# The modulation of a hybrid layer: weight pieces first, all of them split, rows turned by transposition, context and latent tokens loaded behind

## The chip, the cores and the metric

The kernel runs on one core of one Trainium2 chip. The metric is the device time of one execution in microseconds (us), as the median of several runs. Five engines matter here, each with an instruction queue that it works off in order: PE (matmul, with its weight loads shown as PEld), DVE, ACT, POOL and SP. SP issues DMAs; ACT can issue them too, on a queue of its own.

## The reference, cut to what matters

One layer over 2048 latent tokens (`x`) and 256 context tokens (`ctx`), 1024 channels. Everything behind these lines (a gated delta rule in chunks, windowed attention, the merge) is the same before and after.

```python
shift, scale, gate = split(silu(c) @ w_mod + b_mod, 3)        # w_mod 1024 x 3072, float32
shift_c, scale_c, _ = split(silu(c_ctx) @ w_mod + b_mod, 3)
h  = rmsnorm(x, norm_w) * (1 + scale) + shift                 # latent tokens
hc = rmsnorm(ctx, norm_w) * (1 + scale_c) + shift_c           # context tokens
p_c = hc @ w_in[:, :N_STATE]                                  # the state columns of both
p   = h  @ w_in[:, :N_STATE]
```

## The kernel before, in words

**Precision by splitting.** A float32 matrix `w` is cut in two fp32r parts, `hi` (a cast, on ACT or POOL) and `lo = w - hi` (a subtraction on DVE), and the products of the parts are summed in PSUM. A product in plain float32 needs no split, but PE takes two passes for it.

**Start (L60 to L63, L254 to L278).** SP loads the identity (`ident`), then the rows of c, c_ctx, norm_w and b_mod into one 40 x 128 tile (L260). PE turns that tile (L262), DVE copies it to `craw` (L264), ACT takes the tanh (L268) and DVE makes silu of both conditions: `sil4` (hi and lo of the two, four columns) and `silz` (float32).

**Modulation (L303 to L334).** For j = 0 (shift) and j = 1 (scale) come eight pieces `wm` of w_mod, 128 x 1024 float32 (512 KB) each, nine buffers. Six of eight are split: ACT casts `wmh` (L314), DVE subtracts `wml` (L315), PE multiplies `sil4` by both parts (L318, four matmuls of 512 columns). Pieces 3 and 7 (`WHOLE`) go to PE as they are (L310). The products lie in PSUM as four rows (the two conditions by hi, and by lo). ACT and DVE copy them to `mrow` (L325), eight small float32 matmuls against `sel` add the hi and lo rows and turn them to columns (L328), and DVE adds the bias (L330) and makes `modB` (j = 0, L332) and `modA` = (1 + scale) * norm_w (j = 1, L334).

**Context in between.** Behind pieces 4 and 6 of j = 0 the two context tiles are loaded (`load_x`, L283) and normalised (`norm_x`: half the squares on ACT L292, half on DVE L295, a small L296, the power of -0.5 on POOL L72, and the scaling of the tile on DVE L298).

**h (make_h, L336 to L347).** For every two of eight k: PE transposes the normalised tiles (L343), ACT applies modA and modB (L344, `h32`, two buffers), POOL makes the hi part (L346), DVE the lo part (L347).

**State products.** `tm_weights` loads the 272 state columns of w_in in eight pieces (`wr`, 136 KB, three buffers, L364), ACT casts (L365), DVE subtracts (L366). `tm_dense` is 24 matmuls for 128 tokens (L373 to L375) into one of three PSUM buffers. `state_pair` (L428 to L474) takes two such results, normalises and rotates the keys (DVE L433, L437, L438, L442, L457, L461, L464, L465; POOL L72, L451, L460; PE L471) and spills.

**Order of the stage.** First the context: make_h, state_pair. Then eight groups of 256 latent tokens (L490): load two x tiles (four `xt` buffers with the context), norm_x, make_h, tm_dense, state_pair. Then the qkv products begin (L542), and PE is busy until the end. A planner orders each engine's queue when the kernel is built, in program order but with instructions pulled ahead where it expects the earlier ones to wait; `tc.issue_after(r)` keeps the instructions of its block behind `r` in that order. Before, the state weights and the x tiles stand behind the last w_mod piece in this way, and the norms of group 0 behind `rows_out`, the copies of L325.

Of the kernel before, what the change touches and what calls it, by code (L numbers as in the profile page):

```python
# [7 lines left out]
F32 = mybir.dt.float32  # L8
# [9 lines left out]
KT = D // 128  # L18
# [10 lines left out]
def f32(ap):  # L29
    return ap.bitcast(F32)  # L30
# [10 lines left out]
def _hybrid(ctx, tc, nc, V, S, G, T, ins, out, dbg, upto):  # L41
# [19 lines left out]
    dma(ident, ins["k_mats"][0])  # L61
    identr = cst.tile([128, 128], F32R, name="identr")
    V.tensor_copy(identr, ident)  # L63
# [188 lines left out]
    if True:  # L252
# [5 lines left out]
        for r, n, src in ((0, 8, ins["c"]), (8, 8, ins["c_ctx"].rearrange("(o n) -> o n", o=1)),  # L258
                          (16, 8, ins["norm_w"]), (24, 16, ins["b_mod"][:, 0:2 * D])):
            dma(rows[r:r + n], src.rearrange("o (k p) -> (o k) p", p=128))  # L260
# [3 lines left out]
        V.tensor_copy(craw, cols)  # L264
        cc_ = craw[:, 0:16].rearrange("p (c k) -> p k c", c=2)
# [11 lines left out]
        sel = pm.tile([4, 2], F32, name="sel")  # L277
        V.tensor_tensor(sel, ident[0:4, 0:2], ident[0:4, 2:4], op=ALU.add)  # L278

        def load_x(c):  # L280
            xt = px.tile([128, D], F32, name="xt")
            src = ins["ctx"][0, c * 128:(c + 1) * 128] if c < NCB else ins["x"][0, (c - NCB) * 128:(c - NCB + 1) * 128]
            dma(xt, src)  # L283
            return xt
# [15 lines left out]
        pre = []  # L300
        WHOLE = (3, 7)
        modT = pm.tile([128, 16, 2], F32, name="modT")
        for j in range(2):  # L303
            mps = [psum("acc" if n == 0 else "hps", [4, 512], name=f"mps{n}") for n in range(2)]
            for k in range(KT):
                wm = pm.tile([128, D], F32, name="wm", bufs=9)
                wm_dma = dma(wm, ins["w_mod"][0, k * 128:(k + 1) * 128, j * D:j * D + D])
                if k in WHOLE:
                    for n in range(2):
                        T.matmul(mps[n], lhsT=silz[:, k], rhs=wm[:, n * 512:(n + 1) * 512], start=False, stop=k == KT - 1)  # L310
                    continue
                wmh = pm.tile([128, D], F32R, name="wmh", bufs=3)
                wml = pm.tile([128, D], F32R, name="wml", bufs=3)
                S.copy(wmh, wm)  # L314
                V.tensor_tensor(wml, wm, f32(wmh), op=ALU.subtract)  # L315
                for w in (wmh, wml):
                    for n in range(2):
                        T.matmul(mps[n], lhsT=sil4[:, k], rhs=w[:, n * 512:(n + 1) * 512],  # L318
                                 start=k == 0 and w is wmh, stop=False)
                if j == 0 and k in (4, 6):  # L320
                    c = k // 2 - 2
                    pre.append(load_x(c))
                    norm_x(c, pre[c])
            mrow = pm.tile([4, D], F32, name="mrow", tag="wm", bufs=9)
            rows_out = [(V.tensor_copy if n % 2 else S.copy)(mrow[:, n * 512:n * 512 + 512], mps[n]) for n in range(2)]  # L325
            mtp = psum("kt", [128, 8, 2], name="mtp")
            for i in range(8):
                T.matmul(mtp[:, i], lhsT=mrow[:, i * 128:i * 128 + 128], rhs=sel, start=True, stop=True)  # L328
            mt = modT[:, j * 8:j * 8 + 8]
            V.tensor_tensor(mt, mtp, bm[:, j * 8:j * 8 + 8].unsqueeze(2).to_broadcast([128, 8, 2]), op=ALU.add)  # L330
            if j == 0:
                V.tensor_copy(modB, mt)  # L332
            else:
                V.scalar_tensor_tensor(modA, mt, 1.0, nw.unsqueeze(2).to_broadcast([128, KT, 2]), op0=ALU.add, op1=ALU.mult)  # L334

        def make_h(xts, hi, lo, cc):  # L336
            n = len(xts) * 128
            for k in range(0, KT, 2):
                h32 = px.tile([128, 2, 256], F32, name="h32", bufs=2)
                for i in range(2):  # L340
# [3 lines left out]
                    S.activation(h32[:, i, :n], ps[:, :n], AF.Identity, scale=modA[:, k + i, cc:cc + 1],  # L344
# [1274 lines left out]
```

## Time and profile before

| | us |
|---|---|
| median of 3 runs | 1978.22 (1977.2 to 1982.95) |
| the profiled execution's own time | 1983.69 |
| its span (first to last instruction) | 1982.0 |
| granted TensorE clock, mean | 0.993 |
| modA written | 37.50 |
| first state product (tmps) | 39.74 |
| first qkv product (lps) | 133.68 |

How to read it: in the timeline a row has the start, the time from the first start to the last end of the merged instructions, engine, line, operation, output <- inputs, count, and in brackets how long the engine was idle before and what ended that. In the table by stretches each engine has its busy time and the count, then the granted clock of PE, the busy share of the DMA engines and the GB/s.

### The profile page before, as it was taken

To read this page: it belongs to the slowest core of one execution; us is meant where nothing else is said; L and a number is where in the kernel's file an instruction comes from. 1 tells how busy PE (TensorE), PEld (TensorE's weight loads), DVE (VectorE), ACT (ScalarE), POOL (GpSimd) and SP (SyncE) were. 2 spreads that over 40 slices of the span, in tenths; PEclk is the share of its full clock that TensorE was granted. 3 is DMA by queue.
4 is the path that set the end of the run, shared out by engine and by line. 5 is a ranking of instruction groups with operands and counts; after the bars stand their busy time and mean duration, and the time that the engine had idled before them with its cause. 6 is when DMAs were issued, how large, how long until landed. Compare 5 with 4: busy or idle time off the path is not lost. (4 is left out here: it accounts for less than half of the span.)

```text
span 1982.0 us, 32091 instructions
## 1 busy us (share of the span) xinstructions
PE 1911.1 (96%) x10947; PEld 1601.1 (81%) x10947; DVE 1505.9 (76%) x2869; ACT 803.8 (41%) x1994; POOL 706.7 (36%) x768
## 2 busy tenths in 40 slices
PE   7899999999999999999999999999999999999898
PEld 3788888788998787887888888788878888877686
DVE  6979766777776899999778776545786878757888
ACT  5745545554444322211122233324775656532321
POOL 2642111234543201104222333323555343422675
PEclk9999999999999999999999999999999999999999
DMA  7552326765546633537887777755555555455453
GB/s 264 174 139 85 98 88 158 181 169 159 162 145 164 188 111 113 149 97 214 224 244 229 226 222 218 200 162 186 156 181 173 184 164 159 122 174 195 145 168 134
DMA packets 387703, 333.12 MB, mean 168 GB/s; under 512 B 83992, under 2 KB 307536, under 8 KB 386900
## 3 DMA queue, kind: packets, MB, share of 16 engines
q1 hardware_dynamic: 352244, 288.60, 50.0%
q10 hardware_dynamic: 35296, 42.48, 6.2%
q8 instruction: 87, 1.43, 0.3%
q14 instruction: 76, 0.62, 0.1%
HBM read 220.28 MB, written 109.13 MB: 166 GB/s over the span
## 5 line engine op out<-in xcount | busy, mean ns | idle before, releaser
L542 PE MATMUL rps<-hh,wh 128*128 128x512 f32 x768 | 308.9, 402 | 5.4 <-DVE rt L836 4.2
L544 PE MATMUL rps<-hh,wl 128*128 128x512 f32 x768 | 306.8, 400 | 0.0
L543 PE MATMUL rps<-hl,wh 128*128 128x512 f32 x768 | 306.7, 399 | 0.0
L581 DVE SCALAR_TENSOR_TENSOR cacc<-y,cw,cacc 128x512 f32<-128x512 f32 (+1 forms) x224 | 162.7, 747 | 21.6 <-ACT cacc L579 17.8
L542 PEld LDWEIGHTS rps<-hh,wh 128*128 128x128 f32 x768 | 144.9, 189 | 41.1 <-DVE rt L836 5.3
L542 PE MATMUL lps<-hh,wh 128*128 128x512 f32 (+1 forms) x448 | 171.9, 384 | 0.3 <-ACT y L652 0.3
L543 PE MATMUL lps<-hl,wh 128*128 128x512 f32 (+1 forms) x448 | 171.6, 383 | 0.0
L544 PEld LDWEIGHTS rps<-hh,wl 128*128 128x128 f32 x768 | 144.8, 188 | 32.8
L544 PE MATMUL lps<-hh,wl 128*128 128x512 f32 (+1 forms) x448 | 170.9, 382 | 0.0
L543 PEld LDWEIGHTS rps<-hl,wh 128*128 128x128 f32 x768 | 144.8, 189 | 31.6
L962 DVE TENSOR_TENSOR pl<-pt,ph 128x512 fp32r<-128x512 f32 x156 | 105.6, 686 | 45.0 <-ACT ph L960 43.9
L960 ACT CAST ph<-pt 128x512 fp32r<-128x512 f32 x156 | 90.6, 585 | 109.2 <-PE pt L958 71.7
L834 ACT ACTIVATE rt<-rps 128x512 f32<-128x512 f32 x96 | 57.3, 597 | 181.8 <-PE rps L544 158.2
L934 DVE CUSTOM_DVE_ANT_0 pr<-sc,band,sk 128x640 f32<-128x640 f32 (+1 forms) x128 | 106.7, 862 | 19.4 <-PE sc L930 12.1
L944 POOL TENSOR_SCALAR pr<-pr,sm 128x640 f32<-128x640 f32 (+1 forms) x128 | 101.4, 811 | 56.0 <-DVE sm L942 39.2
L765 DVE TENSOR_TENSOR btmp<-N 128x62 f32<-128x62 f32 (+30 forms) x124 | 116.2, 937 | 3.1
L767 DVE TENSOR_TENSOR N<-N,btmp 128x62 f32<-128x62 f32 (+30 forms) x124 | 116.1, 936 | 3.0
L246 DVE TENSOR_TENSOR wl<-wr,wh 128x512 fp32r<-128x512 f32 x120 | 95.2, 806 | 25.6 <-POOL wh L245 24.1
L936 ACT ACTIVATE pr<-pr,sm 128x640 f32<-128x640 f32 (+1 forms) x128 | 104.1, 815 | 23.3 <-DVE sm L934 23.3
L245 POOL TENSOR_SCALAR wh<-wr 128x512 fp32r<-128x512 f32 x72 | 48.6, 689 | 167.4 <-PE lps L543 97.1
L1249 PE MATMUL pps<-yh,wph 128*128 128x512 f32 x256 | 105.4, 414 | 2.3 <-DVE tb L1260 1.7
L1251 PE MATMUL pps<-yh,wpl 128*128 128x512 f32 x256 | 101.4, 397 | 1.6 <-POOL wpl L1211 1.6
(379 smaller groups left out, 5035.4 us busy)
## 6 DMA issues: line engine op xcount, KB each, us to landing
wr<-in_w_in_dram SPq DMA_DIRECT2D x120, 256.0 KB
kw<-Ksp SPq DMA_DIRECT2D x28, 384.0 KB
x<-vsp SPq DMA_DIRECT2D x36, 256.0 KB
k<-ksp SPq DMA_DIRECT2D x34, 256.0 KB
kT<-kTsp SPq DMA_DIRECT2D x34, 256.0 KB
wm<-in_w_mod_dram SPq DMA_DIRECT2D x16, 512.0 KB
xt<-in_x_dram SPq DMA_DIRECT2D x16, 512.0 KB
dtl<-Dsp SPq DMA_DIRECT2D x32, 256.0 KB
```

Source lines behind the costliest of these rows:

```text
L542: T.matmul(ps, lhsT=wh[:, k], rhs=xh[:, k], start=k == 0, stop=False)
L543: T.matmul(ps, lhsT=wh[:, k], rhs=xl[:, k], start=False, stop=False)
L544: T.matmul(ps, lhsT=wl[:, k], rhs=xh[:, k], start=False, stop=k == kt - 1)
L581: V.scalar_tensor_tensor(a, y[:, t:t + n], cw[:, m, t:t + 1], a, op0=ALU.mult, op1=ALU.add)
L765: V.tensor_tensor(tv, A[:, m + 1:, m].unsqueeze(2).to_broadcast([h1 + n, r, m]), A[:, m, 0:m].unsqueeze(1).to_broadcast([h1 + n, r, m]), o ...
L767: V.tensor_tensor(A[:, m + 1:, 0:m], A[:, m + 1:, 0:m], tv, op=ALU.add)
L934: V.tensor_tensor_reduce(s_, ps[:, o:768], band[:, b0:b0 + W + 256], -0.125, sk[:, 1, hd:hd + 1], ALU.add, ALU.min, sm[:, h, 1:2])
L936: S.activation(s_, s_, AF.Exp, scale=-1.0, bias=sm[:, h, 1:2], accum_out=sm[:, h, 2:3])
L944: G.tensor_scalar(p[:, h, :W + 256], p[:, h, :W + 256], sm[:, h, 3:4], 1.0, op0=ALU.mult, op1=ALU.mult)
L962: V.tensor_tensor(pl, pt, f32(ph), op=ALU.subtract)
L1249: T.matmul(ps, lhsT=wh[:, k, ms], rhs=hs[k], start=k == 0, stop=False)
L1251: T.matmul(ps, lhsT=wl[:, k, ms], rhs=hs[k], start=False, stop=k == 3)
```

## The change

- **First issues.** The first w_mod piece is SP's first DMA. The rows of c, c_ctx and norm_w go on ACT's queue; b_mod and the identity follow on SP's, behind the first piece.
- **All pieces split**, but the first half of the very last (float32 product). PE multiplies a piece's hi part at once and its lo part one piece later; `sel` goes.
- **Rows to columns** by eight transpositions against the identity, and DVE adds the hi and lo columns. The 1 of (1 + scale) is added to the bias at the start. The rows of j = 0 are copied out behind the first piece of j = 1, their columns made behind its third.
- **Order of loads.** Context tiles behind the last w_mod piece, the state weights behind the context, x behind the state weights; five `wr` buffers for three.
- **Order of work.** Context norms stand behind the columns of j = 1. The norms of groups 0 and 1 stand behind the second pair of the make_h before (ACT and DVE part), and POOL's turning of the k norm weights behind the last hi part of the context.

The diff, cut (the moved lines of the start are left out):

```diff
+        def load_w(j, k):
+            wm = pm.tile([128, D], F32, name="wm", bufs=9)
+            return wm, dma(wm, ins["w_mod"][0, k * 128:(k + 1) * 128, j * D:j * D + D])
+
+        wm0 = load_w(0, 0)
+        for q, r, n, src in ((adma, 0, 8, ins["c"]), (adma, 8, 8, ins["c_ctx"].rearrange("(o n) -> o n", o=1)),
+                             (adma, 16, 8, ins["norm_w"]), (dma, 24, 16, ins["b_mod"][:, 0:2 * D])):
+            q(rows[r:r + n], src.rearrange("o (k p) -> (o k) p", p=128))
+        dma(ident, ins["k_mats"][0])
...
+        V.tensor_scalar(craw[:, 32:40], craw[:, 32:40], 1.0, None, op0=ALU.add)
...
+        def mod_product(j, k, w, ns=(0, 1), stop=()):
+            for n in ns:
+                T.matmul(mps[j][n], lhsT=(silz if w.dtype == F32 else sil4)[:, k], rhs=w[:, n * 512:(n + 1) * 512],
+                         start=k == 0 and w.name.startswith("wmh"), stop=n in stop)
+        def mod_rows(j):
+            mrow = pm.tile([4, D], F32, name="mrow", tag="wm", bufs=9)
+            for n, copy in enumerate((S.copy, V.tensor_copy)):
+                copy(mrow[:, n * 512:n * 512 + 512], mps[j][n])
+            return mrow
+        def mod_columns(j, mrow):
+            mtp = psum("kt", [128, 8, 4], name="mtp")
+            for i in range(8):
+                T.transpose(mtp[:, i], mrow[:, i * 128:i * 128 + 128], ident[0:4, 0:4])
+            mt = modT[:, j * 8:j * 8 + 8]
+            V.tensor_tensor(mt, mtp[:, :, 0:2], bm[...], op=ALU.add)
+            V.tensor_tensor(modB if j == 0 else mt, mt, mtp[:, :, 2:4], op=ALU.add)
+            if j == 1:
+                V.tensor_tensor(modA, mt, nw[...], op=ALU.mult)
...
             for k in range(KT):
-                if k in WHOLE:
-                    for n in range(2):
-                        T.matmul(mps[n], lhsT=silz[:, k], rhs=wm[:, n * 512:(n + 1) * 512], start=False, stop=k == KT - 1)
-                    continue
...
+                last = j == 1 and k == KT - 1
+                r = slice(512 if last else 0, D)
+                S.copy(wmh[:, r], wm[:, r])
+                V.tensor_tensor(wml[:, r], wm[:, r], f32(wmh[:, r]), op=ALU.subtract)
+                if last:
+                    mod_product(j, k, wm, (0,))
+                    mod_product(*low, stop=(0,))
+                    mod_product(j, k, wmh, (1,))
+                    mod_product(j, k, wml, (1,), (1,))
+                else:
+                    mod_product(j, k, wmh)
+                    if low:
+                        mod_product(*low, stop=(0, 1) if k == 0 else ())
+                    low = j, k, wml
+                if j == 1 and k == 0:
+                    mrow = mod_rows(0)
+                elif j == 1 and k == 2:
+                    mod_columns(0, mrow)
-                if j == 0 and k in (4, 6):
-                    c = k // 2 - 2
-                    pre.append(load_x(c))
-                    norm_x(c, pre[c])
+        mrow = mod_rows(1)
+        mod_columns(1, mrow)
+        for c in range(NCB):
+            with tc.issue_after(wm_dma.ins):
+                pre.append(load_x(c))
+        ctx_dma = x_dma[0]
+        for c in range(NCB):
+            norm_x(c, pre[c])
...
-                wr = pw.tile([128, NST], F32, name="wr", tag="wr", bufs=3)
+                wr = pw.tile([128, NST], F32, name="wr", tag="wr", bufs=5)
...
-        with tc.issue_after(wm_dma.ins):
+        with tc.issue_after(ctx_dma.ins):
             wh, wl = tm_weights(C_ST, NST)
...
-                with tc.issue_after(wm_dma.ins):
+                with tc.issue_after(wr_dma[0].ins):
                     xts.append(load_x(c))
                 with ExitStack() as behind:
-                    if gi == 0:
-                        for r in rows_out:
-                            behind.enter_context(tc.issue_after(r.ins))
+                    if gi < 2:
+                        for h in made[:2]:
+                            behind.enter_context(tc.issue_after(h.ins))
                     norm_x(c, xts[j])
```

More of the change, by code (lines that the diff above doesn't have):

```diff
@@ L276, in _hybrid @@
         V.tensor_copy(silz[:, :, 0:2], silc)
-        sel = pm.tile([4, 2], F32, name="sel")
-        V.tensor_tensor(sel, ident[0:4, 0:2], ident[0:4, 2:4], op=ALU.add)
+        x_dma = [None]
         def load_x(c):
@@ L298, in norm_x @@
             V.tensor_scalar(xt, xt, rstd[:, c:c + 1], None, op0=ALU.mult)
-        pre = []
-        WHOLE = (3, 7)
         modT = pm.tile([128, 16, 2], F32, name="modT")
+        mps = [[psum("acc" if n == 0 else "hps", [4, 512], name=f"mps{n}") for n in range(2)] for j in range(2)]
+        def mod_product(j, k, w, ns=(0, 1), stop=()):
+            for n in ns:
+                T.matmul(mps[j][n], lhsT=(silz if w.dtype == F32 else sil4)[:, k], rhs=w[:, n * 512:(n + 1) * 512],
+                         start=k == 0 and w.name.startswith("wmh"), stop=n in stop)
@@ L303, in _hybrid @@
+        low = None
         for j in range(2):
-            mps = [psum("acc" if n == 0 else "hps", [4, 512], name=f"mps{n}") for n in range(2)]
             for k in range(KT):
-                wm = pm.tile([128, D], F32, name="wm", bufs=9)
-                wm_dma = dma(wm, ins["w_mod"][0, k * 128:(k + 1) * 128, j * D:j * D + D])
-                if k in WHOLE:
-                    for n in range(2):
-                        T.matmul(mps[n], lhsT=silz[:, k], rhs=wm[:, n * 512:(n + 1) * 512], start=False, stop=k == KT - 1)
-                    continue
+                wm, wm_dma = load_w(j, k) if j + k else wm0
+                last = j == 1 and k == KT - 1
+                r = slice(512 if last else 0, D)
@@ L312, in _hybrid @@
                 wmh = pm.tile([128, D], F32R, name="wmh", bufs=3)
                 wml = pm.tile([128, D], F32R, name="wml", bufs=3)
[L314 to L319, printed above, removed]
-                if j == 0 and k in (4, 6):
-                    c = k // 2 - 2
-                    pre.append(load_x(c))
-                    norm_x(c, pre[c])
@@ L324, in _hybrid @@
[L324 to L334, printed above, removed]
+                S.copy(wmh[:, r], wm[:, r])
[10 more added lines that the diff above has]
+                    low = j, k, wml
@@ L343, in make_h @@
                         T.transpose(ps[:, j * 128:(j + 1) * 128], xt[:, (k + i) * 128:(k + i + 1) * 128], ident)
[L344 to L347 removed]
+                    h = S.activation(h32[:, i, :n], ps[:, :n], AF.Identity, scale=modA[:, k + i, cc:cc + 1],
+                                     bias=modB[:, k + i, cc:cc + 1])
+                hi_ = G.tensor_scalar(hi[:, k:k + 2], h32[:, :, :n], 1.0, 1.0, op0=ALU.mult, op1=ALU.mult)
+                lo_ = V.tensor_tensor(lo[:, k:k + 2], h32[:, :, :n], f32(hi[:, k:k + 2]), op=ALU.subtract)
+                if k == 2:
+                    made = [h, lo_]
+            made.append(hi_)
+            return made
         pm_.__exit__(None, None, None)
```

30 lines of the change are left out of this document (14 added, 16 removed).

## The prediction

> **What bounds the kernel now.** I read the page's engine shares first, then the busy times by stretches, then the timeline of the first 50 us. The page's PE row and the stretches:
>
> ```profile
> PE 1911.1 (96%) x10947; PEld 1601.1 (81%) x10947; DVE 1505.9 (76%) x2869; ACT 803.8 (41%) x1994; POOL 706.7 (36%) x768
> ```
>
> ```profile
> 0.00:7.00 7.00, 0.30 (x1) 0.18 (x1) 1.37 (x11) 1.99 (x3) 0.20 (x4) 1.00 0.51 164
> 7.00:26.00 19.00, 16.21 (x62) 5.44 (x63) 13.91 (x20) 11.91 (x16) 1.14 (x2) 1.00 1.03 411
> 26.00:37.50 11.50, 10.21 (x44) 3.78 (x42) 8.72 (x19) 6.01 (x14) 0.93 (x1) 1.00 0.63 216
> 37.50:50.00 12.50, 11.65 (x77) 10.69 (x78) 9.45 (x20) 8.35 (x20) 8.85 (x13) 0.86 0.44 130
> 50.00:112.00 62.00, 53.88 (x402) 47.68 (x400) 58.24 (x141) 45.58 (x129) 43.03 (x52) 0.99 0.52 170
> 112.00:134.00 22.00, 21.15 (x152) 20.78 (x152) 13.73 (x41) 10.66 (x32) 11.98 (x15) 0.86 0.43 133
> 134.00:1982.00 1848.00, 1797.74 (x10217) 1512.58 (x10215) 1400.49 (x2623) 719.33 (x1788) 640.52 (x683) 1.00 0.57 166
> ```
>
> The columns are PE, PEld, DVE, ACT, POOL, clock, DMA share, GB/s. Four limits follow each other. From 7 to 26 the DMA engines are full (1.03, 411 GB/s). From 50 to 112, the groups of latent tokens, DVE is busy 58.24 of 62. From 112 to 134 PE is the busy one, part of the time at a lower clock. Behind 134 PE works 97% of the time and the change touches nothing: whatever the qkv products' start (L542) moves is the gain. So the question is not how much sooner modA is ready, but how much of that still stands after DVE's full stretch.
>
> **The front, DMA.** Timeline of the start:
>
> ```profile
> 2.68 2.54 SPq L307 DMA_DIRECT2D wm<-in_w_mod_dram  x5
> 4.10 0.30 PE L262 MATMUL cols<-ident,rows 40*128 40x40 f32 x1 [4.10 <-DMA rows<-in_b_mod_dram]
> 5.55 0.18 DVE L273 TENSOR_TENSOR sil<-silc,sil 128x16 fp32r<-128x16 f32 x1
> 6.51 1.04 ACT L314 CAST wmh<-wm 128x1024 fp32r<-128x1024 f32 x1 [1.62 <-DMA wm<-in_w_mod_dram]
> 27.06 1.05 ACT L314 CAST wmh<-wm 128x1024 fp32r<-128x1024 f32 x1 [0.22 <-DMA wm<-in_w_mod_dram]
> 28.71 1.15 ACT L365 CAST wh<-wr 128x272 fp32r<-128x272 f32 x3 [0.60 <-DMA wr<-in_w_in_dram]
> ```
>
> ACT's cast waits for its piece at 6.51 (the first) and at 27.06 (piece 6 of j = 1). Between lie 16 transfers of 512 KB, 14 pieces and the two context tiles: 20.55 / 16 = 1.28 us each. The last piece so landed at 28.3. After: SP's first DMA is the first piece, which I put where the identity's stands now (0.81):
>
> ```profile
> 0.81 0.39 SPq L61 DMA_DIRECT2D ident<-in_k_mats_dram  x1
> ```
>
> That is 1.87 sooner than 2.68, so the piece lands at 6.51 - 1.87 = 4.64. Fifteen more come without context between: 4.64 + 15 x 1.28 = 23.9; the identity (64 KB, an eighth of a piece, 0.16) stands behind the first: the last piece lands at 24.1, 4.2 sooner. ACT needs no more than 1.05 a piece.
>
> The identity and the bias rows now queue behind the first piece. If they land with it at about 4.8 instead of 4.1, the turned rows, the tanh (ahead of the first cast on ACT) and `sil4` come 0.7 later: ACT's first cast starts near 5.6 (6.51 before) and DVE's first subtraction near 6.75. The Trainium skill speaks against the first edit here: "DMA: Bandwidth & Descriptors", section "Issuing engines are not separate DMA queues", says that DMAs of several issuing engines run on the same 16 DMA engines and interleave, and that issuing from more than one saves only issue time. By that the three rows on ACT's queue share the engines with the first piece and gain nothing; no run here shows such a start yet, and the sum takes no gain for them.
>
> **The front, DVE and PE.** Two pieces more in j = 0 and one and a half in j = 1 are split: 3.5 subtractions.
>
> ```profile
> 23.05 0.17 DVE L330 TENSOR_TENSOR modT<-mtp,craw 128x16 f32<-128x16 f32 x1 [1.19 <-PE mtp L328]
> 23.27 0.17 DVE L332 COPY modB<-modT 128x16 f32<-128x16 f32 x1
> 23.35 6.90 DVE L315 TENSOR_TENSOR wml<-wm,wmh 128x1024 fp32r<-128x1024 f32 x6
> 32.14 1.88 PE L310 MATMUL mps<-wm,silz 128*4 128x512 f32 x4
> 33.95 1.94 PE L328 MATMUL mtp<-sel,mrow 4*128 4x2 f32 x16
> 34.05 0.68 DVE L325 COPY mrow<-mps 4x512 f32<-4x512 f32 x1 [2.67 <-PE mps L310]
> 37.50 0.16 DVE L334 SCALAR_TENSOR_TENSOR modA<-modT,craw 128x16 f32<-128x16 f32 x1
> 37.70 1.93 ACT L344 ACTIVATE h<-hps,modB,modA 128x256 f32<-128x256 f32 x4 [1.60 <-DVE modA L334]
> ```
>
> Six subtractions run in 6.90: 1.15 each, just under the 1.28 of a transfer. So DVE holds the pace but has no slack: 15.5 x 1.15 = 17.8, plus 0.68 and two times 0.17 for j = 0, is 18.8 from 6.75, to 25.6. That is the DMA's end too (24.1 + half a cast 0.5 + half a subtraction 0.6 = 25.2). From there: the last matmul 0.3, the copy of a half row 0.68, the transpositions (eight, where L328 is 16 passes in 1.94; half of the eight wait for the copy: 0.6), three small DVE operations at 0.2 with 0.15 to start: modA stands near 28.0 instead of 37.66. Two float32 products of 1.88 go, only a half is left, and it runs while the last half is cast: no term.
>
> **The context is now late next.** Its tiles land behind the last piece, at 25.4 and 26.7.
>
> ```profile
> 12.89 0.63 ACT L292 ACTIVATE junk<-xt 128x512 bf16<-128x512 f32 x1
> 15.63 0.75 DVE L298 TENSOR_SCALAR xt<-xt,rstd 128x1024 f32<-128x1024 f32 x1 [0.69 <-POOL rstd L72]
> ```
>
> A norm took 12.89 to 16.38, 3.5 us. So the second tile is ready at 30.2, a little later since the columns of j = 1 want DVE at the same time; with the transposition the first h comes at 31.0, against 37.70: **6.7 sooner**. That is the most the front gives.
>
> **What DVE then has to do in addition.** Before, most of the state weights' split and the norms of group 0 were done under the modulation's wait:
>
> ```profile
> 30.16 1.14 DVE L366 TENSOR_TENSOR wl<-wr,wh 128x272 fp32r<-128x272 f32 x3
> 34.66 0.67 DVE L295 SCALAR_TENSOR_TENSOR junk<-xt 128x512 bf16<-128x512 f32 x1
> 35.45 0.21 DVE L296 TENSOR_SCALAR ss<-ss 128x1 f32<-128x1 f32 x1
> 36.27 0.43 DVE L366 TENSOR_TENSOR wl<-wr,wh 128x272 fp32r<-128x272 f32 x1
> 37.58 0.79 DVE L366 TENSOR_TENSOR wl<-wr,wh 128x272 fp32r<-128x272 f32 x2
> 38.46 0.75 DVE L298 TENSOR_SCALAR xt<-xt,rstd 128x1024 f32<-128x1024 f32 x1
> ```
>
> ```profile
> L298 DVE TENSOR_SCALAR xt<-xt,rstd x18: 742/989/1110, 15.6 to 109.1; 128x1024 f32<-128x1024 f32 x18
> ```
>
> At the first h only the second scaling (0.75) and four of eight `wl` (one of them running) were left. After, the x tiles land last and both norms are still to come: 2 x (0.67 + 0.21 + 0.75) less 0.75 is 2.5; where POOL is at work the scaling takes up to 1.11 instead of 0.75, so 2.5 to 3.2. One or two `wl` more (0.4 each) make 3.5 to 4 in all. DVE idled 12.5 - 9.45 = 3.05 between 37.5 and 50; most of that were waits between h, POOL and `hl` that return, and I let it take up a third, 1.1. Left: 6.7 - 3.8 + 1.1 = **4.0**.
>
> A second count, over all of DVE until it stops being the limit. Before: idle 112 - (1.37 + 13.91 + 8.72 + 9.45 + 58.24 = 91.69) = 20.3. After: 5.4 until the first subtraction (6.75 less 1.37 of work), none in the stream, 1 until the first h, 1 to 2 until group 0, 3.8 as before in the groups: about 11.7. Added work: 3.5 x 1.15 = 4.0 and 1 for small adds and slower scalings. The shift is 20.3 - 11.7 - 5.0 = 3.6. Both say about 4.
>
> When x lands is the third check. Before:
>
> ```profile
> 38.04 0.33 SPq L364 DMA_DIRECT2D wr<-in_w_in_dram  x1
> 40.81 8.99 SPq L283 DMA_DIRECT2D xt<-in_x_dram  x3
> 44.52 0.63 ACT L292 ACTIVATE junk<-xt 128x512 bf16<-128x512 f32 x1 [0.54 <-DMA xt<-in_x_dram]
> 45.32 1.02 ACT L344 ACTIVATE h<-hps,modB,modA 128x256 f32<-128x256 f32 x2
> ```
>
> Issue to landing is 3.7. The last three `wr` need released buffers, so SP reaches x near 32; the tiles land at 35.7 and 37.0, are normed by 40.5, and group 0's first h comes near 40.7, against 45.32: 4.6 sooner. It fits. The wait that the change adds on SP (x behind `wr`) holds the small rotary loads and spills behind it too; none of them is wanted before the context's state products are through.
>
> So 1974.2: the profiled execution (1983.69, span 1982.0) would be 1979.7 in this sum; it stands 5.5 above the median of the runs, 1978.22, and I take the difference over.
>
> **The rivals.** *More than that.* DVE's idle time takes up all the added work and the 6.7 stands: 1971.5. For it speaks that DVE's share from 37.5 to 50 is only 76%; against it the 94% after. Beside it stands a lower PE clock:
>
> ```profile
> 112.58 0.60 PE L373 MATMUL tmps<-wh,hh 128*128 128x272 f32 x1 [1.56 <-DVE xn L442]
> ```
>
> ```profile
> 112.00:118.00 6.00, 5.42 (x24) 5.42 (x25) 4.01 (x11) 2.27 (x6) 2.57 (x4) 0.50 0.35 112
> 118.00:120.00 2.00, 2.00 (x18) 2.00 (x18) 1.08 (x4) 0.62 (x3) 0.73 (x2) 1.00 0.06 21
> ```
>
> PE waited for PSUM buffers, and then ran 24 matmuls in 5.42 (0.226 each) at clock 0.50, where two us later 18 took 2.00 (0.111): 24 x 0.115 = 2.8 lost where PE is the limit. Another order of the groups can spare it (4.0 + 2.8: 1971.4; both, 1968.7) or make a second one. The Trainium skill ("TensorE: Matmul & The Clock Gate", "What's actually happening") gives a half clock after an idle window of about 3.4 us and full clock again after as long a busy one; the 0.50 after the sparse stretch agrees. Chance of over 5.9 gained in either way: 0.34.
>
> *Nothing reaches PE.* POOL's part in the scalings and the waits h, POOL, `hl` swallow the rest, or DVE falls behind in the stream by the 0.13 that it has: 1976.2 to 1979.7, say 1977.5. For it speaks that DVE is full for 62 us whatever comes first. Here belongs too that the planner's order undoes the early issue. 0.12.
>
> *Slower: x waits for the state weights.* If the planner puts `wl` on DVE behind the context's `hl`, the last `wr` is issued near 38, as now (38.04), x only behind it: landing at 42 and 43.3, normed at 46.8, group 0's h at 47.0, 1.7 later than now; with 0.7 for scalings beside POOL 1980.6. It decides from a second x tile landing at 41.6 on, and it passes 0.3% when that comes at 46.9 or later. Five buffers speak against it. 0.08, of which 0.06 over 0.3%.
>
> **How the numbers follow.** 0.3% is 5.9 us, about what a measurement of this kernel can tell from no change. The forecast, a gain of 2.0 to 5.9 (its own range 1972.3 to 1976.2), has 0.46. Faster: 0.34. Slower: 0.06. Within: 0.46 + 0.12 + 0.02 = 0.60. The range leaves out the deepest part of the first rival and most of the last: 1968.0 to 1980.0.
>
> **What would show it.** The last split cast of ACT near 24.1 instead of 27.06; modA near 28.0; first h near 31.0; group 0's first h near 40.7; the first qkv product near 129.7 instead of 133.68. The forecast is wrong if DVE's busy share until group 0 leaves more than 3 us idle (then x is late), if the clock dip at 112 moves or goes, or if the stretch behind 134 changes length by itself:
>
> ```profile
> 133.68 0.28 PE L542 MATMUL lps<-hh,wh 128*128 128x256 f32 x1
> ```

## The result, and the profile after

The kernel after takes 1985.76 us (median of 22 runs), the kernel before 1980.88 in the same series; the ratio is 1.0023, 95% interval 1.0014 to 1.0032: 4.6 us slower (2.8 to 6.3) where 4 us of gain were forecast. Single executions far outside their series (one of after at 9024.06 us, the profiled one of e4 at 3699.72) are left out of the ratios and of the profile figures below. The profiled execution of after took 1982.79 us with a span of 1981.0, so this one execution is 0.9 shorter than the profiled one of before while the medians say the opposite. The trace tells where time went up to the qkv products; only the medians tell how much it was in all.

The busy times of after by the stretches that the prediction showed of before (PE, PEld, DVE, ACT, POOL, granted clock, DMA share, GB/s):

```profile
0.00:7.00 7.00, 0.29 (x1) 0.18 (x1) 1.84 (x7) 2.45 (x3) 0.20 (x4) 1.00 0.68 219
7.00:26.00 19.00, 17.27 (x64) 5.22 (x64) 16.77 (x22) 15.25 (x17) 0.00 (x0) 1.00 1.03 411
26.00:37.50 11.50, 7.03 (x30) 3.09 (x28) 9.07 (x24) 6.70 (x19) 2.75 (x3) 0.73 0.60 187
37.50:50.00 12.50, 11.09 (x71) 10.08 (x69) 7.12 (x15) 6.62 (x19) 6.94 (x12) 0.84 0.45 147
50.00:112.00 62.00, 54.22 (x361) 48.62 (x360) 53.94 (x136) 41.59 (x116) 41.10 (x49) 0.89 0.50 162
112.00:134.00 22.00, 21.32 (x171) 19.94 (x169) 16.93 (x44) 13.97 (x39) 13.97 (x17) 1.00 0.34 105
134.00:1982.00 1848.00, 1800.77 (x10243) 1515.94 (x10242) 1410.47 (x2632) 720.94 (x1792) 638.74 (x686) 0.99 0.57 166
```

Read the DVE column from 50 to 112 first: 58.24 before, 53.94 now. The engine that the prediction held for the limit of the groups is no longer full. PE is as busy as before there (53.88 and 54.22), with 41 matmuls fewer (402 and 361): the clock went from 0.99 to 0.89, and from 26 to 50 it is at 0.73 and 0.84. So the groups of latent tokens now wait for something else, and PE does a part of its work there at half clock.

The timeline of after, the front and the first two groups:

```profile
4.43 1.04 ACT L340 CAST wmh<-wm 128x1024 fp32r<-128x1024 f32 x1 [1.04 <-DMA wm<-in_w_mod_dram]
5.49 0.29 PE L268 MATMUL cols<-ident,rows 40*128 40x40 f32 x1 [5.49 <-DMA ident<-in_k_mats_dram]
5.50 1.23 DVE L341 TENSOR_TENSOR wml<-wm,wmh 128x1024 fp32r<-128x1024 f32 x1
7.75 0.18 DVE L280 TENSOR_TENSOR sil<-silc,sil 128x16 fp32r<-128x16 f32 x1
7.85 1.05 ACT L340 CAST wmh<-wm 128x1024 fp32r<-128x1024 f32 x1 [0.76 <-DMA wm<-in_w_mod_dram]
...
20.52 7.50 DVE L341 TENSOR_TENSOR wml<-wm,wmh 128x1024 fp32r<-128x1024 f32 x7
25.79 0.62 ACT L340 CAST wmh<-wm 128x512 fp32r<-128x512 f32 x1 [0.23 <-DMA wm<-in_w_mod_dram]
30.72 0.75 DVE L305 TENSOR_SCALAR xt<-xt,rstd 128x1024 f32<-128x1024 f32 x1 [0.47 <-POOL rstd L70]
31.59 0.78 DVE L402 TENSOR_TENSOR wl<-wr,wh 128x272 fp32r<-128x272 f32 x2
32.38 0.79 DVE L402 TENSOR_TENSOR wl<-wr,wh 128x272 fp32r<-128x272 f32 x2
33.08 0.75 DVE L305 TENSOR_SCALAR xt<-xt,rstd 128x1024 f32<-128x1024 f32 x1
33.74 0.43 DVE L402 TENSOR_TENSOR wl<-wr,wh 128x272 fp32r<-128x272 f32 x1
34.10 0.17 DVE L330 TENSOR_TENSOR modA<-modT,craw 128x16 f32<-128x16 f32 x1
35.03 0.56 ACT L374 ACTIVATE h<-hps,modB,modA 128x256 f32<-128x256 f32 x1
...
33.38 0.90 SPq L290 DMA_DIRECT2D xt<-in_x_dram  x2
39.56 0.63 ACT L299 ACTIVATE junk<-xt 128x512 bf16<-128x512 f32 x1 [1.64 <-DMA xt<-in_x_dram]
47.64 0.56 ACT L374 ACTIVATE h<-hps,modB,modA 128x256 f32<-128x256 f32 x1 [0.87 <-PE hps L373]
49.61 0.65 ACT L299 ACTIVATE junk<-xt 128x512 bf16<-128x512 f32 x1
63.34 0.58 ACT L374 ACTIVATE h<-hps,modB,modA 128x256 f32<-128x256 f32 x1
137.21 0.28 PE L579 MATMUL lps<-hh,wh 128*128 128x256 f32 x1
```

The lead over before shrinks, turns, and grows the other way: modA 3.40 sooner (34.10 for 37.50), the first h 2.67 sooner (35.03 for 37.70), group 0's first h 2.32 later (47.64 for 45.32), group 1's first h (63.34) some 10 later, and the first qkv product 3.53 later (137.21 for 133.68). Group 1's first h before, near 53, is the second of the three in this row (each group has eight):

```profile
52.59 1.49 ACT L344 ACTIVATE h<-hps,modB,modA 128x256 f32<-128x256 f32 x3
```

From the first qkv products on, the queues of both kernels hold the same instructions in the same order on every engine.

The stretch from modA to the first qkv product, which the rest is about, as one row of before and one of after:

```profile
37.50:133.68 96.18, 86.36 (x624) 78.85 (x625) 81.11 (x199) 64.41 (x175) 63.86 (x78) 0.95 0.49 157
```

```profile
34.10:137.21 103.11, 91.86 (x628) 82.83 (x628) 82.12 (x206) 66.30 (x180) 64.50 (x79) 0.90 0.48 156
```

It is 6.93 longer. PE is busy 5.50 longer, for four matmuls more, and idle 1.43 longer (11.25 for 9.82). The granted clock can account for the busy part: the clock records of these two traces hold 1.00 and 0.50 and nothing between, so a mean of 0.95 over 96.18 is 9.6 us at half clock, and 0.90 over 103.11 is 20.6; work that fills 11 us more at half clock takes 5.5 us longer for it. DVE has 1.0 more to do and 5.9 more of idle time. So in these two executions the sum is: front -3.4, stage +6.9, first qkv product +3.5.

### The profile page after: what moved, and what is told of

It reads as the page before. It is cut to its first block, busy times and chain, and to the rows that moved or that the text cites. A ratio compares the mean times of both kernels' runs of the same rounds, so it can differ in the third digit from the quotient of the medians.

```text
span 1981.0 us, 32066 instructions
## 1 busy us (share of the span) xinstructions
PE 1912.0 (97%) x10931; PEld 1603.1 (81%) x10931; DVE 1516.2 (77%) x2874; ACT 807.5 (41%) x1998; POOL 703.7 (36%) x768
## 3 DMA queue, kind: packets, MB, share of 16 engines
q8 instruction: 87, 1.43, 0.3%
## 5 line engine op out<-in xcount | busy, mean ns | idle before, releaser
L981 POOL TENSOR_SCALAR pr<-pr,sm 128x640 f32<-128x640 f32 (+1 forms) x128 | 101.3, 814 | 55.4 <-DVE sm L979 36.7
```

The source lines that it names most:

```text
L981: G.tensor_scalar(p[:, h, :W + 256], p[:, h, :W + 256], sm[:, h, 3:4], 1.0, op0=ALU.mult, op1=ALU.mult)
```

## The experiments

The theory that I came to, in steps, is this: the planner sees a front with other times and loads, gives the first groups **another order**, and in that order the stage behind modA takes longer than what the front gains. Its rivals: the front's time does not carry to the end at all; one part of the change (the hold-back of group 1's norms, the hole at the start, the x loads behind the state weights, PE's lost clock) carries the loss alone. Where an expectation names a theory by a letter, it says what the theory is; C is that the front's time carries to the end, B in e13 and e14 that it is swallowed, O that the order decides.

All runs in one table; stage is from modA to the first qkv product, behind is the rest of the span, in the profiled execution of each; the ratio is to before in the same series (in the row of e5 and e11 it is that of e5, since e11 was one execution). Time of one execution varies: before was profiled three times, 1848.3, 1839.0 and 1844.4 behind the first qkv product.

| | modA | stage | first qkv | behind | ratio (95%) |
|---|---|---|---|---|---|
| before, three profiles | 37.5, 37.5, 37.5 | 96.2, 95.3, 96.6 | 133.7, 132.8, 134.1 | 1848.3, 1839.0, 1844.4 | 1 |
| after, two profiles | 34.1, 33.3 | 103.1, 101.3 | 137.2, 134.6 | 1843.8, 1852.5 | 1.0023 (1.0014 to 1.0032) |
| e1 modulation only | 35.2 | 102.3 | 137.5 | 1850.6 | 1.0054 (1.0038 to 1.0070) |
| e2 loads only | 38.0 | 101.0 | 139.0 | 1844.6 | 1.0034 (1.0013 to 1.0056) |
| e3 rows first | 34.2 | 101.4 | 135.6 | 1851.5 | 1.0035 (1.0022 to 1.0049) |
| e4 x behind the context | | | | | 1.0025 (1.0013 to 1.0037) |
| e5, e11 group 1 free | 33.4, 33.9 | 99.3, 98.9 | 132.7, 132.8 | 1849.0, 1847.6 | 1.0029 (1.0016 to 1.0041) |
| e6 no hold-back | 33.7 | 104.2 | 137.8 | 1847.7 | 1.0023 (1.0011 to 1.0036) |
| e7 modA first | 30.1 | 108.4 | 138.4 | 1841.0 | 1.0033 (1.0020 to 1.0046) |
| e8 added matmuls | 34.0 | 109.4 | 143.5 | 1850.6 | 1.0066 (1.0047 to 1.0086) |
| e13 before, 6 loads ahead | 44.1 | 96.2 | 140.3 | 1847.0 | 1.0042 (1.0026 to 1.0058) |
| e14 after, 3 loads ahead | 38.4 | 100.5 | 138.9 | 1852.9 | 1.0047 (1.0029 to 1.0066) |
| e15 three edits together | 30.7 | 100.5 | 131.2 | 1849.3 | 1.0015 (1.0000 to 1.0031) |
| e16 before, 1 load ahead | 40.7 | 102.5 | 143.2 | 1850.4 | 1.0058 (1.0037 to 1.0079) |
| e17 before, 4 loads ahead | 43.7 | 102.5 | 146.1 | 1847.1 | 1.0072 (1.0052 to 1.0092) |
| e18 before, five wr buffers | 37.5 | 97.0 | 134.5 | 1843.4 | 0.9998 (0.9985 to 1.0010) |

**e1 and e2: each half of the change alone.** e1 is after with the load order and hold-backs of before, e2 is before's modulation with the loads and hold-backs of after.

```diff
 e1, on after
+                if j == 0 and k in (4, 6):
+                    c = k // 2 - 2
+                    pre.append(load_x(c))
+                    norm_x(c, pre[c])
...
-                wr = pw.tile([128, NST], F32, name="wr", tag="wr", bufs=5)
+                wr = pw.tile([128, NST], F32, name="wr", tag="wr", bufs=3)
...
-                    if gi < 2:
-                        for h in made[:2]:
-                            behind.enter_context(tc.issue_after(h.ins))
+                    if gi == 0:
+                        for r in rows_out:
+                            behind.enter_context(tc.issue_after(r.ins))
 e2, on before: the same lines the other way
```

> The changed kernel with the loads and the order of work as before: context tiles loaded and normed behind pieces 4 and 6 of j = 0, three wr buffers, state weights and x behind the last w_mod piece, norms of group 0 behind the copies of the rows, no other norms held back. Theory L (the order of the loads costs the time: x behind the state weights reaches group 0 late): modA earlier than 37.5, group 0's first h earlier than 45.3, first qkv product at 130 to 133, and the kernel 1 to 3 us faster than before. Rival S (the stream of pieces is what fails: all pieces split leaves DVE no slack): first qkv product at 134 or later, no gain or slower.

> The kernel before with its own start and modulation (pieces 3 and 7 whole, columns by products), but context behind w_mod, state weights behind the context, x behind them, five wr buffers, norms of groups 0 and 1 and the turned k norm weights held back as in the changed kernel. Theory L: group 0's first h two us or more later than 45.3, PE at half clock for a time between 45 and 65, first qkv product at 137 to 141, 4 to 7 us slower than before. Rival S: first qkv product within 1 us of 133.7, no change.

Each half alone is slower than before, e1 by 10.7 us and e2 by 6.7 (ratio less 1, times 1980). So it isn't the loads that spoil a good modulation, nor the other way: the theory that only one of them carries the loss falls. e1 has modA 2.3 us sooner than before and the first qkv product 3.9 later.

**e3 and e4: the hole at the start, and the x loads.** e3 puts the identity and the rows ahead of the first piece again, all on SP's queue. e4 lets x go behind the context's tiles, not behind the state weights.

```diff
 e3, on after
-        wm0 = load_w(0, 0)
-        for q, r, n, src in ((adma, 0, 8, ins["c"]), (adma, 8, 8, ins["c_ctx"].rearrange("(o n) -> o n", o=1)),
...
-        dma(ident, ins["k_mats"][0])
+        dma(ident, ins["k_mats"][0])
+        for q, r, n, src in ((dma, 0, 8, ins["c"]), (dma, 8, 8, ins["c_ctx"].rearrange("(o n) -> o n", o=1)),
...
+        wm0 = load_w(0, 0)
 e4, on after
-                with tc.issue_after(wr_dma[0].ins):
+                with tc.issue_after(ctx_dma.ins):
                     xts.append(load_x(c))
```

> The changed kernel, but the identity and the four row loads on SP's queue ahead of the first w_mod piece, as before. The second piece then lands 1.3 us behind the first instead of 3.4, and the conditions are ready before DVE's first subtraction. Theory L: modA moves by less than 1.5 us, the first qkv product stays at 136 to 138, still 3 to 5 us slower than before. Rival S: the stream ends up to 2 us sooner and the first qkv product with it, at 135 or earlier.

> The changed kernel, but the x tiles are held back behind the context tiles only, not behind the last state weight, so that SP need not wait for the wr buffers before it issues them. Theory L: the first x tile is issued near 25 instead of 33.4 and landed by 31, group 0's first h comes at 45 or earlier instead of 47.6, the first qkv product at 132 to 134.5, time from 2 us faster to 1 us slower than before. Rival S: x earlier, but group 0's h and the first qkv product move by less than 1 us, still 3 to 5 us slower than before.

The timeline of e3, its first two casts:

```profile
6.67 1.04 ACT L340 CAST wmh<-wm 128x1024 fp32r<-128x1024 f32 x1 [1.92 <-DMA wm<-in_w_mod_dram]
7.92 1.05 ACT L340 CAST wmh<-wm 128x1024 fp32r<-128x1024 f32 x1 [0.21 <-DMA wm<-in_w_mod_dram]
```

With the rows ahead the pieces come 1.25 apart, where in after the second cast began 3.42 behind the first. The second piece comes at the same time in both, modA too (34.23 and 34.10): issuing the first piece first gained nothing, and lost nothing. e4 has the time of after, so the wait of x for the state weights isn't the loss either. The profile of e4 is of the execution left out above, so it shows only that x is now issued ahead of the last three state weights, not how much sooner it comes.

**e5, e6, e11: the hold-backs.**

```diff
 e5 and e11, on after
-                    if gi < 2:
+                    if gi < 1:
 e6, on after
-                    if gi < 2:
+                    if gi < 0:
-        wn = norm_w(pa, "k_norm_w", made[2])
+        wn = norm_w(pa, "k_norm_w")
```

> The changed kernel, but only the norms of group 0 stand behind the make_h before; those of group 1 are free again. Theory H (holding the norms of group 1 back makes its h late, and PE runs dry and falls to half clock behind group 0): group 1's first h near 54 instead of 63.3, no half clock between 54 and 63, the first qkv product at 132 to 135, 2 to 5 us faster than the changed kernel. Rival P (the groups take the time that DVE and PE need, whatever the order): group 1's first h earlier, but the first qkv product within 1 us of 137.2, time as the changed kernel.

> The changed kernel with nothing held back: norms of groups 0 and 1 and the turned k norm weights free. Theory H: at least as good as with group 1 free, first qkv product at 131 to 135, 2 to 6 us faster than the changed kernel. Rival P: first qkv product within 1 us of 137.2. If the norms of group 0 now stand ahead of the context's hl on DVE, the context's last h comes later than 42.7.

> The changed kernel with the norms of group 1 free, profiled a second time. Its first qkv product came at 132.7, a microsecond sooner than in the kernel before, though its median was 4.9 us above. Theory A: 132.7 was a lucky clock; this time PE falls to half clock at another place and the first qkv product comes at 135 to 139. Rival B: 132.7 again within 1 us, and the loss of this kernel lies behind the qkv products' start, where its order differs from that of the kernel before.

Busy times of after from 52 to 60, then of e5:

```profile
52.00:56.00 4.00, 1.81 (x11) 1.17 (x9) 3.93 (x16) 2.40 (x7) 3.88 (x5) 0.88 0.58 215
56.00:60.00 4.00, 4.00 (x18) 4.00 (x19) 3.37 (x9) 0.62 (x1) 1.71 (x3) 0.50 0.00 0
```

```profile
52.00:56.00 4.00, 3.68 (x28) 3.46 (x29) 3.55 (x11) 3.14 (x8) 1.77 (x4) 1.00 0.25 99
56.00:60.00 4.00, 4.00 (x36) 4.00 (x36) 3.53 (x8) 3.53 (x12) 3.28 (x4) 1.00 0.15 42
```

In after the norms of group 1 begin at 49.61, as the hold-back says, so PE has little to multiply from 52 to 56 (1.81 of 4); then the clock goes to 0.50 and 18 matmuls take the time of 36. In e5 group 1's first h stands at 54.74 instead of 63.34, there is no dip here, and the first qkv product comes at 132.69, and again at 132.80: 4.5 sooner than in the first profile of after and 1.9 sooner than in the second, 1.0 sooner than in the first of before. The place and the cause of this dip are so shown. But the time didn't follow, 1.0029: what e5 gains up to the qkv products is not seen in its medians. Its queues also differ from those of before behind them; e18 comes back to that. In e6, without any hold-back, group 1's h is as early (54.35) and the first qkv product as late as in after (137.84): being early in one group is not enough.

**e7: modA first.** The state weights' splits and the context's scalings stand behind modA on DVE.

```diff
+                with tc.issue_after(modA_i[0].ins):
+                    V.tensor_tensor(wl[:, k, :n], wr[:, :n], f32(wh[:, k, :n]), op=ALU.subtract)
...
+            with tc.issue_after(modA_i[0].ins):
+                V.tensor_scalar(xt, xt, rstd[:, c:c + 1], None, op0=ALU.mult)
```

> The changed kernel, but on DVE the split of the state weights and the scalings of the tiles stand behind the operation that writes modA, so that modA no longer waits behind them in DVE's queue. modA should come at 30.5 to 31.5 instead of 34.1, the first h not before the second context tile is scaled, 33 to 34.5 instead of 35.0. Theory H: the first qkv product moves by less than 1 us, time as the changed kernel. Rival F (what counts is how soon the first h comes): the first qkv product 1 to 2 us sooner, and time 1 to 2 us less.

Its row of the stage:

```profile
30.06:138.43 108.37, 94.28 (x633) 83.09 (x634) 88.35 (x215) 67.14 (x183) 67.53 (x82) 0.91 0.49 157
```

modA came 4.0 sooner than in after, the first h 2.2 (32.84), and the first qkv product 1.2 later. DVE has 6.2 us more to do behind modA (88.35 for 82.12). Of these 3.5 are the five `wl` splits and the two scalings that stood ahead of modA; they make the stage longer, not its end later. Another 2.2 are three splits of the qkv weights (`wl`, 512 columns) that in after come behind the first qkv product: the order changed here as well. An early modA by itself is worth nothing here.

**e8: is it the clock alone?** Five matmuls are added ahead of each of the sixteen rounds of transpositions in groups 0 and 1 (80 in all); their results are overwritten.

```diff
+                    for _ in range(fill):
+                        T.matmul(ps[:, :NST], lhsT=identr, rhs=wh[:, 0], start=True, stop=True)
```

> The changed kernel with work added: five matmuls of 272 columns ahead of the transpositions of each h tile of groups 0 and 1, 80 in all, written to PSUM and overwritten there, to keep PE busy where it waits. They take 80 x 0.125 = 10 us at full clock. Theory C (the half clock of PE behind group 0 is what makes the groups late): granted clock between 54 and 63 at 1.0 instead of 0.5 to 0.7, group 1's first h sooner than 63.3, and the first qkv product no later than 137.2 though PE has 10 us more to do. Rival: the clock rises but the first qkv product comes 2 to 6 us later, since PE has no such slack.

The clock stayed at 1.00 between 54 and 63, and the first qkv product came at 143.45, 6.2 later than in after. The added work cost more than the clock that it kept; as a test of the clock it is inconclusive.

**e9, e10, e12: one more execution each** of before, after and before, unchanged.

> The kernel before, profiled a second time. Theory A (the change's loss lies ahead of the qkv products, where the queues differ; behind them all engines have the same order): first qkv product again at 133.7 within 1 us; the span from there to the end differs from 1848.3 by up to 4 us, which is the spread of the runs. Rival B (the loss lies behind): first qkv product spreads by 3 us or more by itself.

> The changed kernel, profiled a second time. Theory A: modA again at 34.1 and the first qkv product at 137.2, both within 1 us, PE at half clock between 54 and 63 again. Rival B: the first qkv product moves by 3 us or more between two executions.

> The kernel before, profiled a third time, for the spread. Theory A: first qkv product at 133.7 within 1 us. Rival B: a spread of 3 us or more.

They took 1973.52, 1988.83 and 1980.26 us. The stage repeats within 1.3 us for before and 1.9 for after (with modA 0.8 sooner, e10 has its first qkv product 2.7 sooner than after, where 1 was expected); the part behind it varies by 9 us in both, though the order there is the same. So the 4.6 us of the medians can't be split between the two parts from single profiles.

**e13 and e14: pure delays.** Loads of 512 KB that nobody reads are issued ahead of the rest: six in before, three in after. The planned order stays but for two matmuls in e13 and six places in e14.

```diff
 e13, on before (e16: range(1), e17: range(4)); e14: range(3), on after, ahead of load_w(0, 0)
+        for p in range(6):
+            dma(pm.tile([128, D], F32, name="wm", bufs=9), ins["w_mod"][0, p * 128:(p + 1) * 128, 2 * D:3 * D])
```

> The kernel before with six 512 KB loads that nobody reads (pieces of the third part of w_mod) issued ahead of the rows; the planned order of all engines stays that of before (two matmuls change places). All of the front comes six transfers later, 6 x 1.28 = 7.7 us. Theory C (time of the front carries to the end one for one, so that the change could have gained, and its loss lies in the stage behind): the first qkv product near 141.4 and the time 7.7 above before, 1.0039. Theory B (the stage of the groups has slack that swallows the front's time, DVE being full whatever comes first): less than 3 us above before, under 1.0015.

> The kernel after with three such loads ahead of the first piece; the planned order is that of after (six places differ). The front comes 3.8 us later. Theory C: 3.8 above after, so 8.5 above before, 1.0043. Theory B: as after, 4.7 above before, 1.0024.

The row of the stage in e13:

```profile
44.08:140.26 96.18, 86.57 (x625) 78.76 (x625) 80.89 (x199) 64.13 (x175) 64.62 (x78) 0.95 0.50 157
```

modA stood 6.58 later than in before, the stage took 96.18 as in the profile of before, and the time is 8.3 above before (5.2 to 11.5; expected 7.7). In e14 the time is 9.3 above before (5.7 to 13.1; expected 8.5); its profile is less clear, with modA 4.3 later than in the first one of after and the first qkv product 1.7 later (5.1 and 4.3 against the second). A delay of the front **does** carry to the end where the order is kept, one for one as far as the intervals can tell. The theory that DVE's full stretch swallows it falls.

**e15: the repairs together**: the edits of e3, e5 and e7 on after.

> The kernel after with the three single edits together: identity and rows ahead of the first piece on SP; modA ahead of the wl splits and of the context's scalings on DVE; the hold-back of the norms for group 0 only. Its start has no hole, modA should stand near 29, the first h near 32, group 1's first h near 54. If the front's time carries (theory C) and the hold-back is the loss, the first qkv product comes near 130 and the time is 2 to 4 us below before, 0.998 to 0.999. Theory O (it is the order that the planner gives to the first groups and the first qkv products, and nearly any order but the one of before costs some us): 1.002 to 1.005 again, whatever the front does.

Its row of the stage:

```profile
30.70:131.15 100.45, 87.46 (x633) 79.66 (x633) 85.48 (x213) 65.89 (x182) 67.77 (x81) 0.95 0.48 157
```

The first qkv product came at 131.15, the earliest of all, 2.5 before that of before (130 was expected). The stage took 100.45, 4.3 more than in before. The clock is that of before (0.95), and so is DVE's idle time (15.0 and 15.1); the 4.4 us that DVE has more to do behind modA make up the difference. Up to here the prediction's sum holds: 6.8 sooner, less the added work, is 2.4. But the time is 3.0 above before (0.0 to 6.1), not 2 to 4 below. It is the best of the versions with the change and beats neither kernel by what can be measured; if the other executions were like this one up to the first qkv product, what it lost, it lost behind it.

**e16 and e17: the same program in another order.** One load ahead, or four, makes the planner choose another order for before, the same one in both cases.

> The kernel before with one such load ahead of the rows: the front is 1.3 us later and nothing else of the program changes, but the planner gives a different order from it (TensorE's differs up to its 3500th instruction, far into the qkv products). Theory C: 1.3 above before, 1.0007. Theory O: 4 to 10 above before, 1.002 to 1.005, as with the other kernels of another order.

> The kernel before with four unread loads ahead of the rows; its planned order is that of the kernel with one such load, in every queue, and not that of before. Front 4 x 1.28 = 5.1 us later than before. Theory O with C (the order sets the length of the stage from modA to the first qkv product, the front's time is added one for one): stage 102.5 as with one load (before 96.2), first qkv product near 147, time 3.8 above the kernel with one load: 16 above before, 1.008. If the stage of the kernel with one load was an accident of its execution: stage near 96, 5.1 above before, 1.0026.

The rows of the stage, e16 and e17:

```profile
40.72:143.23 102.51, 89.99 (x624) 81.42 (x625) 86.22 (x204) 64.64 (x175) 65.47 (x80) 0.90 0.48 155
```

```profile
43.66:146.12 102.46, 90.07 (x625) 81.36 (x625) 86.47 (x204) 64.85 (x175) 65.50 (x80) 0.90 0.49 155
```

Two executions with different delays, and the stage is 102.5 both times, 6.3 longer than in before, where the six loads of e13 left it at 96.18. With one load, which costs 1.3 of DMA time, modA comes 3.2 later, the first qkv product 9.6, and the run takes 11.5 us more (7.3 to 15.6). With four it takes 14.3 more (10.3 to 18.2; expected 16). But for the unread loads nothing was added to the work, and six of them did no harm to the stage: it's the order. PE's row looks like that of after: clock 0.90, 3.6 us more busy, 2.7 more idle. DVE has 5.1 us more to do in this stage (86.22 for 81.11). In part it is work taken ahead from behind the first qkv product: four splits of the qkv weights for one, 1.7 us. In part the same work takes longer: the 36 subtractions for `hl` take 29.6 us, 27.4 in before.

**e18: five buffers alone.**

```diff
 on before
-                wr = pw.tile([128, NST], F32, name="wr", tag="wr", bufs=3)
+                wr = pw.tile([128, NST], F32, name="wr", tag="wr", bufs=5)
```

> The kernel before with five wr buffers for three and nothing else, one of the edits of the change; the planner's order differs from the fourth state weight on, up to TensorE's 2100th instruction. modA is hardly moved (37.5). Theory O: the stage from modA to the first qkv product is 99 to 104 us and the time 3 to 9 above before, 1.0015 to 1.0045. Otherwise (the size of the buffer is a small help, the order neutral): stage near 96, within 2 us of before.

```profile
37.50:134.51 97.01, 89.36 (x625) 81.34 (x625) 81.55 (x199) 64.22 (x173) 66.89 (x79) 0.91 0.46 147
```

Another order again, and the time is that of before. So the strong form, that nearly any other order costs, falls; some do and some don't. The row also warns of the clock: 0.91 and 3.0 us more of busy PE, as in the slower kernels, but PE is idle 2.2 less, and the stage is only 0.8 longer. Here the time at half clock went for the most part into time in which PE had been idle.

e18 says something of e5, e11 and e15 too. Behind the first qkv product the traces of all four show the same order on every engine (but for the place of single instructions). Yet e18 has the time of before, while e5, whose first qkv product comes 1.8 us sooner, takes 6.1 us more than e18 by the ratios, whose intervals do not meet (0.9985 to 1.0010, 1.0016 to 1.0041); and from that product to the end the profiles give 1843.4 for e18 and 1849.0, 1847.6 and 1849.3 for the others. So these versions with the change lose some microseconds behind the first qkv product, and neither the stage nor the order behind it is the reason. No run here shows what is.

## Why the prediction was wrong

**The step that failed is the sum "Left: 6.7 - 3.8 + 1.1 = 4.0", with the second count, "The shift is 20.3 - 11.7 - 5.0 = 3.6. Both say about 4".** Both treat the groups as a fixed pile of DVE work with "3.8 as before in the groups" of idle time. That figure became 8.1 from 50 to 112 (62 - 53.94): the stage had another order and hold-backs, and PE went to half clock for 11 us more. Term by term, from the first h to the first qkv product in the profiled executions: the first h came 2.7 sooner and not 6.7; DVE had 0.6 more to do and not 3.8, since the norms did add some 3 us there, but one `wl` split had left and `hl` and the key operations took some 2 us less; and DVE's idle time, of which 1.1 was to go, grew by 5.7. That makes -3.5, the wrong sign (-0.9 in the second profile of after, with 3.4, 0.6 and 3.7). With its first term alone put right the sum would have said no change; the loss came with the idle time. The stage is 6.9 longer in after (5.1 in its second profile), and 6.3 longer in e16 and e17, where but for unread loads only the order changed. That the order is what lengthened it in after too is argued from these, and shown in after itself only for the hold-back of group 1 (e5). The principle of the sum was right as far as it went: e13 and e14 show that a delay of the front arrives where the order is kept, and in e15, where DVE's idle time is that of before, the sum comes out at the first qkv product.

**The front, but for its first term, was too hopeful.** The first piece was cast at 4.43 (4.64 forecast), and the pieces come 1.28 apart later; but the second came 3.42 behind the first, where 1.28 and 0.16 for the identity were counted, and the last cast came at 25.79, not near 24.1. The rows landed late as well: the turning of the rows began at 5.49, and `sil` was ready at 7.93. The Trainium skill's rule, weighed in the prediction ("DMA: Bandwidth & Descriptors", "Issuing engines are not separate DMA queues"), was the better guide: rows, identity and first pieces share the engines, and e3, which has all of it on one queue and the rows ahead, casts the second piece within 0.07 of the same time.

**DVE in the stream**: seven subtractions, the last a half one, in 7.50 are the pace that was foreseen, with no slack to win back the start: they ended at 28.02, not 25.6.

**modA, "near 28.0"**, came at 34.10. 2.4 of that are the subtractions. The rest is DVE's queue: two scalings of the context, five `wl` splits and the norms' squares stand ahead of modA, where the sum had "three small DVE operations at 0.2". e7 shows its size: with splits and scalings behind it modA stands at 30.06.

**The first h 6.7 sooner** became 2.7 sooner. **x**: issued at 33.38 ("near 32"), but the first tile was read at 39.56, 6.2 behind the issue and not 3.7; group 0's first h came at 47.64 and not 40.7. The wait of more than 3 us that the prediction named as the sign of it is in the row from 37.5 to 50: DVE idles 12.5 - 7.12 = 5.4.

**The rivals.** "Nothing reaches PE" had the front swallowed; e13 rules that out for the order of before. "x waits for the state weights" has the right place, group 0's h at 47.0 (47.64 measured), but, by the times, not the cause of the loss: e4 unties x and stays at 1.0025. The one that happened stood in half a sentence of the first rival, that another order "can spare it ... or make a second one", priced only on the side of gain. The list of what would prove the forecast wrong did name the moved clock dip.

**What stays open.** In the two profiles of after the first qkv product comes 3.5 and 0.9 later than in the first of before, and the ratio is worth 4.6. Between 1 and 4 us lie behind the qkv start or in the spread of executions, 9 us wide there, with the same order in the queues. e5, e11 and e15 show that a loss behind the qkv start is no mere chance of the profiles: something that the versions with the change have in common, and that no run isolates, may cost there in after as well. The prediction's premise, "whatever the qkv products' start (L542) moves is the gain", is so far not safe. Nor is it settled which edges of the order cost how much: the hold-back of group 1 was located (e5), but taking it away doesn't bring the time of before. A version with the front of after and the order of before wasn't tried.

## What to carry to other kernels

Where a planner orders the queues from estimated times, a change at the front is also a change of the order behind it: compare the planned queues before pricing the front, and price the new order as a rival of its own, on both sides. A neutral delay that keeps the order (e13) tells in one run what a microsecond of the front is worth, and one that upsets it (e16) tells what an order can cost; here 1 to 1 within the interval, and some 8 us at the first qkv product (9.6 less the 1.3 of the load itself). A sum over the busiest engine holds only as long as its waits for the others, PE's clock included, keep their times. And the median has the last word: e5 and e15 reached the first qkv product sooner than before and were no faster.

## What the runs showed of the hardware

**Half clock without a long idle stretch.** The busy times of after around the dip, in windows of some 3.4 us:

```profile
48.20:51.65 3.45, 2.92 (x16) 1.92 (x17) 1.57 (x3) 3.45 (x12) 1.54 (x2) 1.00 0.41 109
51.65:55.05 3.40, 2.05 (x11) 1.40 (x11) 3.40 (x12) 2.03 (x5) 2.93 (x4) 1.00 0.75 275
55.05:58.50 3.45, 2.61 (x12) 2.61 (x13) 3.38 (x10) 0.93 (x3) 2.00 (x4) 0.50 0.00 0
58.50:61.90 3.40, 3.40 (x17) 3.40 (x17) 0.87 (x3) 0.41 (x1) 0.66 (x1) 0.50 0.02 5
```

From the timeline of PE, its longest wait there:

```profile
55.89 0.59 PE L409 MATMUL tmps<-wh,hh 128*128 128x272 f32 x1 [0.98 <-POOL hh L376]
```

PE was busy 2.05 of the 3.40 us ahead of the dip, and never idle for more than 0.98. The Trainium skill ("TensorE: Matmul & The Clock Gate", "What's actually happening") speaks of an idle window of about 3.4 us; the length agrees (0.50 in two windows of it, from 55.05 to 61.90), but no such idle window is seen: the window ahead of this dip was 60% busy.

**Loads at the start.** SP's first issues in after:

```profile
0.81 0.39 SPq L259 DMA_DIRECT2D wm<-in_w_mod_dram  x1
1.25 0.41 SPq L264 DMA_DIRECT2D rows<-in_b_mod_dram  x1
1.71 0.42 SPq L265 DMA_DIRECT2D ident<-in_k_mats_dram  x1
2.17 5.15 SPq L259 DMA_DIRECT2D wm<-in_w_mod_dram  x8
```

A 512 KB piece issued first and one issued 1.36 us later, with four small loads and 64 KB between, were cast 3.42 apart; with the same loads ahead of both, 1.25 apart. **Spread.** Executions of one kernel with one order differ by 9 us of 1845 behind the qkv start (1839.0 to 1848.3 for before).
